# Memory attention of a hybrid streaming layer: scores and prompt values as three float32r passes, the query norm as the exponential's scale

## The chip, the cores and the metric

The kernel runs on one core of a Trainium2 chip. The metric is the device time of one execution in microseconds (us). Shares, windows and chains come from one execution taken by the hardware profiler, whose own time stands beside its span below. Five engines work side by side, each through an instruction stream of its own: PE (TensorE: matrix products and transposes; its weight loads, PEld, are recorded apart), DVE (VectorE), ACT (ScalarE), POOL (GpSimd) and SP (SyncE, which issues the loads and stores). Products are written to banks in PSUM, eight in all; the other engines copy them out to SBUF.

## The reference

One layer serves a prompt of 512 tokens and a sample of 64 tokens with the same weights: a mixer (a gated delta recurrence beside differential attention), then attention over a memory, then a feed-forward part. The change lies in the memory attention:

```python
def _rmsnorm(x, g):
    xf = x.astype(jnp.float32)
    y = xf * lax.rsqrt(jnp.mean(xf * xf, axis=-1, keepdims=True) + EPS)
    return (y * g.astype(jnp.float32)).astype(x.dtype)
...
def _mem_kv(mem, g, wk, wv):
    B, M, _ = mem.shape
    m = _rmsnorm(mem, g)
    return (m @ wk).reshape(B, M, H_MEM, D_MEM), (m @ wv).reshape(B, M, H_MEM, D_MEM)

def _mem_attn(x, mk, mv, wq, wo):
    B, L, _ = x.shape
    q = (x @ wq).reshape(B, L, H_MEM, D_MEM)
    s = jnp.einsum('blhd,bmhd->bhlm', q.astype(jnp.float32), mk.astype(jnp.float32)) * (D_MEM ** -0.5)
    p = jax.nn.softmax(s, axis=-1)
    o = jnp.einsum('bhlm,bmhd->blhd', p, mv.astype(jnp.float32)).astype(x.dtype)
    return o.reshape(B, L, D_MODEL) @ wo
...
    h = x + jnp.concatenate([oa, ob], axis=-1) @ p['w_out']
    h = h + _mem_attn(_rmsnorm(h, p['ln_mem_q']), mem_k, mem_v, p['w_mem_q'], p['w_mem_o'])
    hn = _rmsnorm(h, p['ln_ffn'])
    h = h + jnp.square(jax.nn.relu(hn @ p['w_ff1'])) @ p['w_ff2']
```

The model width is 1024, the memory has 256 tokens, and four heads are 256 wide, so the scores are divided by 16. The prompt attends to memory keys and values that are projected here from `mem_prompt` (they are outputs too). The sample attends to cached ones, `cache_mem_k` and `cache_mem_v`.

## The kernel before

Activations are kept transposed, features on the 128 partitions and the 576 tokens (512 of the prompt, then 64 of the sample) along the free axis. A large tile is a "pair", `u` in the profile: 128 x 2 x 4 x 576 elements. It either holds the high and the low half of one split operand for 512 features, or two unrelated things, which `view` cuts out. `pair(slot)` hands out one of six slots (0 to 5); a slot's next tile waits until the last reader of the one before it is done.

**Split operands.** A large projection is not done in float32 but as three float32r products: the operand is rounded to float32r (the high half), the rest is a float32r number again (the low half), and high x high, high x low and low x high are summed in one bank. For weights `split_weights` (L154) loads a raw block, ACT casts the high half `wh` (L160), DVE subtracts for the low half `wl` (L161). There are three raw buffers and two each of `wh` and `wl`, so weights are split one block ahead of their use. For activations `split_to` (L196) does the same, with a gain per feature as ACT's scale where there is one (L203).

**Projections.** `project` (L168) makes 128 output columns for all tokens in two halves, tokens 0 to 255 and 256 to 575. Per 128 input features the first half takes one 512-wide product of the high weights with the high and low halves of the activations side by side, and one 256-wide product of the low weights; the second half takes three products of 320. Over 1024 features that is 8 x (512 + 256) and 24 x 320 columns. Since the first half leaves its two parts in two halves of a bank, its readout adds them: `add_to` (L192) copies one on ACT (L193) and adds the other on DVE (L194).

**Banks** (L74): three for projections (`pr`), two for transposes and short work (`ba`), one each for `g0`, `g1` and `gs`. Scores use `gs` alone, so the scores of the next tile wait until the exponential of the tile before has read them.

**Around the memory attention,** in program order:
- L1028 to L1058: memory keys and values are projected for 256 memory tokens, in two blocks of 512 columns each. `mkv` holds transposed keys `mkT` and values `mv`, in float32. Keys go to a token-major buffer `mkt` first (L1045), are transposed on PE and copied to `mkT` by ACT (L1054); values go to `mv` directly. Both are stored by DMA from where they stand (L1055).
- L1064 to L1110: the mixer's output projection adds to the residual (`add_residual`, L1071); squares are summed, and at the end `norm_columns` (L1098) makes five columns of inverse roots of the mean squares, one for each tile of 128 queries, by a power on POOL (L207). The gain of the norm is already in the split activations `hx` (L1108), the root is not.
- L1111 and L1112: the root must multiply every query. `row_broadcast` (L209) turns the five columns into a row of 576 on all partitions, `rB`, by five float32 products with the identity (ten records) and two copies. It is handed to the first query projection and put between its two halves (`between`).
- L1115 to L1126: cached keys (`cm`, 1 MB, L1116) and cached values (`cmv`, 1 MB, L1119) are loaded, values first in the built order; the keys are transposed in four groups of four through `ba` and copied to `cmT`, which shares a pair with `cmv`.
- L1128 to L1175: four heads. For each, two query projections with readout `scaled` (query times `rB`, L1137) into `qh`. Then five query tiles: four of the prompt and one that ends on the 64 sample tokens. A tile takes two float32 score products (L1149), maximum along the row on DVE (L1151), times -1/16 (L1152), exponential on ACT with the maximum as bias, 1/16 as scale and the row sum as second output (L1154), reciprocal and scaling on DVE (L1155, L1156), two transposes on PE (L1159), and a copy of each block into `pT`, one by ACT (L1160), one by DVE (L1161). After the five tiles come the values: two float32 products of 512 columns and two of 64 for each of two output blocks, and the split of the results into `mo` (L1174, L1175).
- L1177 on: the output projection of the memory attention, the second norm (with a row of roots of its own before the feed-forward part), and the feed-forward part.

**What sets the order.** The program order above is not the order on the engines. A scheduler places each engine's instructions when the kernel is built, by priority and by when their operands are ready in its own estimate; each engine then runs its list in order and waits at each instruction for what it needs. So the query projections of head h+1 are interleaved with the score tiles and the values of head h, and the output projection with those of head 3. Weight splits have high priority. The entries of the broadcast are pinned. Loads and stores are issued by SP in one queue, in its built order.

In the profile every product stands at L106 (`mm`), every transpose at L112 (`tr`), so tiles tell them apart: `pr` is a projection, `gs` scores, `g` values, `ba` transposes and the broadcast. A float32 product or transpose leaves two records.

## Time and profile before

| what | before |
|---|---|
| median of 3 runs | 1047.21 us (1047.1 to 1047.5) |
| the profiled execution's own time | 1047.51 us |
| its span in the trace | 1045.8 us |
| granted TensorE clock, mean | 0.997 |
| DMA, whole span | 89.96 MB at a mean of 86 GB/s |
| projections' products on high weights | 2680 records, 692.6 us busy |
| projections' products on low weights | 1776 records, 484.5 us busy |
| casts of weights (ACT) and subtractions (DVE) | 153 each, 136.5 and 157.3 us busy |

The profile's page gives busy time by engine, then groups by line, then the chain of work that ended last, followed back from the last instruction. Busy times of neighbouring PE instructions overlap: a record's duration holds its filling and draining, so the distance from one start to the next, the pitch, says what an instruction costs, not its mean duration. The span is 1.7 us shorter than the execution's own time. Views of the trace are given as rows that begin with a time in us from the span's start and a duration; what stands in brackets at the end is the idle time just before and what ended it.

### The profile page before, as it was taken

What the parts mean: (1) busy time and instruction counts of PE and PEld (TensorE: products, weight loads), DVE (VectorE), ACT (ScalarE), POOL (GpSimd) and SP (SyncE); (2) the same over time, 40 slices, a digit from 0 to 9 for tenths busy, and PEclk for the clock granted to TensorE, in tenths of its full rate; (3) what the DMA queues carried; (4) which work ended last, traced back from release to release, by engine and by line L of the source; (5) the groups of instructions that cost most, each with busy time, mean ns of one, the idle gap of its engine ahead of it and who ended that gap; (6) DMA issues with size and microseconds to landing.
All of it is one profiled execution on the core that took longest, in us unless ns stands there. A gap on an engine that the chain in (4) does not pass through costs nothing.

```text
span 1045.8 us, 16809 instructions
## 1 busy us (share of the span) xinstructions
PE 1027.9 (98%) x6520; PEld 928.9 (89%) x6520; DVE 669.1 (64%) x1473; ACT 434.7 (42%) x905; POOL 58.0 (6%) x124
## 2 busy tenths in 40 slices
PE   9999999999999999999999999999999999999996
PEld 7989899998888878998877899999999999999996
DVE  6676784766667675664554666666666666666773
ACT  6644664433465674343333443323232222222344
POOL 3431110100000000000000000000000000000000
PEclk9999999999999999999999999999999999999998
DMA  7432411100321446434111232141413131323312
GB/s 210 129 104 81 122 43 26 37 21 21 92 64 56 157 136 207 135 86 137 41 41 41 67 92 65 48 120 45 121 48 114 51 112 57 108 58 112 92 51 91
DMA packets 139442, 89.96 MB, mean 86 GB/s; under 512 B 5522, under 2 KB 130576, under 8 KB 138852
## 3 DMA queue, kind: packets, MB, share of 16 engines
q1 hardware_dynamic: 138996, 88.24, 28.8%
q8 instruction: 52, 0.85, 0.4%
q10 hardware_dynamic: 368, 0.66, 0.2%
q14 instruction: 26, 0.21, 0.1%
HBM read 79.14 MB, written 9.74 MB: 85 GB/s over the span
## 4 chain that ended last, share of the span: by engine, by line
PE 67%; issue 2%; DVE 0%; ACT 0%; POOL 0%; POOLq 0%; ACTq 0%
PE pr L106 58%; PE g L106 3%; PE gs L106 3%; PE ba L112 2%; PE ba L106 0%; ACT u L1240 0%; POOL tiny L207 0%; DVE u L1076 0%; POOL ta L207 0%; POOLq L1320 0%; DVE an L1008 0%; DVE u L1175 0%; DVE on L779 0%; ACT u L1174 0%; ACT p L1154 0%
## 5 line engine op out<-in xcount | busy, mean ns | idle before, releaser
L106 PE MATMUL pr<-u,wh 128*128 128x320 f32 (+2 forms) x2680 | 692.6, 341 | 1.3 <-DVE p L322 1.0
L106 PEld LDWEIGHTS pr<-u,wh 128*128 128x128 f32 x2680 | 456.8, 188 | 36.2 <-DVE p L322 1.3
L106 PE MATMUL pr<-u,wl 128*128 128x256 f32 (+1 forms) x1776 | 484.5, 300 | 0.0
L106 PEld LDWEIGHTS pr<-u,wl 128*128 128x128 f32 x1776 | 327.1, 189 | 8.1 <-issue 1.4
L160 ACT CAST wh<-raw 128x1024 fp32r<-128x1024 f32 (+1 forms) x153 | 136.5, 892 | 234.9 <-PE pr L106 222.7
L161 DVE TENSOR_TENSOR wl<-raw,wh 128x1024 fp32r<-128x1024 f32 (+1 forms) x153 | 157.3, 1028 | 59.9 <-ACT wh L160 56.8
L1076 DVE TENSOR_TENSOR u<-u,pr 128x256 f32<-128x256 f32 (+1 forms) x160 | 72.4, 453 | 62.5 <-PE pr L106 59.7
L200 ACT CAST u<-p 128x256 fp32r<-128x256 f32 x64 | 27.8, 434 | 51.8 <-DVE p L1194 51.8
L207 POOL TENSOR_TENSOR tiny<-tiny,nhalf 128x1 f32<-128x1 f32 (+4 forms) x11 | 9.4, 852 | 651.4 <-DVE tiny L1256 409.0
L106 PE MATMUL pr<-wh,u 128*128 128x512 f32 x128 | 41.1, 399 | 0.0
L201 DVE TENSOR_TENSOR u<-p,u 128x256 fp32r<-128x256 f32 x64 | 29.2, 457 | 15.1 <-ACT u L200 15.1
L193 ACT COPY p<-pr 128x256 f32<-128x256 f32 (+1 forms) x42 | 15.6, 372 | 49.1 <-PE pr L106 49.1
L1078 DVE TENSOR_TENSOR u<-u,pr 128x256 f32<-128x256 f32 x80 | 33.6, 420 | 2.4
L194 DVE TENSOR_TENSOR p<-pr,p 128x256 f32<-128x256 f32 (+1 forms) x42 | 17.8, 423 | 25.5 <-ACT p L193 25.4
L456 DVE SCALAR_TENSOR_TENSOR p<-p,gcol,p 128x579 f32<-128x579 f32 x33 | 27.1, 821 | 9.0 <-ACT p L454 8.5
L1193 DVE TENSOR_TENSOR p<-pr,rB 128x320 f32<-128x320 f32 x32 | 15.7, 492 | 25.9 <-PE pr L106 25.9
L1194 DVE SCALAR_TENSOR_TENSOR p<-p 128x256 f32<-128x256 f32 x64 | 29.3, 458 | 2.2
L203 ACT ACTIVATE u<-u,gcol 128x256 fp32r<-128x256 f32 (+1 forms) x32 | 17.0, 533 | 31.1 <-DVE u L1078 31.1
L106 PE MATMUL g<-u,qz 128*128 128x256 f32 (+4 forms) x96 | 29.3, 409 | 0.0
L741 ACT COPY X<-g 128x512 f32<-128x512 f32 (+1 forms) x24 | 13.2, 551 | 34.3 <-PE g L112 34.3
L106 PEld LDWEIGHTS pr<-wh,u 128*128 128x128 f32 x128 | 23.4, 188 | 4.4
L106 PE MATMUL gs<-u,aT 128*128 128x128 f32 (+1 forms) x136 | 26.6, 320 | 0.0
(336 smaller groups left out, 1194.1 us busy)
## 6 DMA issues: line engine op xcount, KB each, us to landing
raw<-in_w_ff_dram SPq DMA_DIRECT2D x32, 512.0 KB
raw<-in_w_ff_dram SPq DMA_DIRECT2D x64, 256.0 KB
raw<-in_w_in_dram SPq DMA_DIRECT2D x28, 512.0 KB
raw<-in_w_mem_k_dram SPq DMA_DIRECT2D x8, 512.0 KB
raw<-in_w_mem_v_dram SPq DMA_DIRECT2D x8, 512.0 KB
raw<-in_w_out_dram SPq DMA_DIRECT2D x8, 512.0 KB
raw<-in_w_mem_q_dram SPq DMA_DIRECT2D x8, 512.0 KB
raw<-in_w_mem_o_dram SPq DMA_DIRECT2D x8, 512.0 KB
```

What stands on the lines that cost most here:

```text
L106: i = nc.tensor.matmul(out, lhsT, rhs, start=start, stop=stop)
L112: i = nc.tensor.transpose(out, in_, ident[:n, :n])
L160: A.copy(wh, raw)
L161: V.tensor_tensor(wl, raw, wh.bitcast(F32), ALU.subtract)
L194: V.tensor_tensor(dst, b, dst, ALU.add)
L200: A.copy(h, src)
L201: V.tensor_tensor(lo, src, h.bitcast(F32), ALU.subtract)
L203: A.activation(h, src, AF.Identity, scale=g)
L456: V.scalar_tensor_tensor(yv[:, :n], cb[:, i : i + n], cwt[:, m, i : i + 1], yv[:, :n], ALU.mult, ALU.add)
L1076: V.tensor_tensor(hm, hm, b, ALU.add)
L1078: V.tensor_tensor(hm, hm, more, ALU.add)
L1194: V.scalar_tensor_tensor(f, f, 0.0, f, ALU.max, ALU.mult)
```

## The change

- **Keys and prompt values are split.** The pairs of `mkv` and `cmu` become float32r. Transposed keys of the prompt and of the cache are rounded by ACT and their rest subtracted by DVE (`split_turned`). The low halves of the prompt's keys lie in small tiles that the recurrent stage used (`At0`, `At1`, `Dt0`, `Dt1`), those of the cached keys in the second half of `cmu`. The prompt's values are copied from the token buffer to `mv` (high) and subtracted into four tiles (`Y0`, `Y1` and two of `B1`). Keys and values now both pass through one token buffer, `tokens`.
- **Queries are split and not scaled.** `split_query` adds the two parts of the first half into a short-lived tile `zr`, copies the high half on ACT to `qh` and subtracts the low half on DVE into `ql`.
- **The root goes into the exponential.** The five columns are multiplied by 1/16 and by -1/16 once (`grow16`, `shrink16`). The maximum of a tile is multiplied by its column of `shrink16`, and the exponential takes its column of `grow16` as scale, by a pointer. `row_broadcast` and `rB` go from this stage; the one before the feed-forward part stays.
- **Scores** are six float32r products a tile in place of two float32 ones, for the sample's tile as well.
- **Probabilities** of the prompt are split from the transposes' bank: high by ACT, low by DVE, four instructions where there were two copies. The sample's go to a tile `pS` by one DVE copy and stay float32.
- **Values:** six float32r products of 512 columns per output block in place of two float32 ones; the sample's two products of 64 columns stay float32, against cached values that are now loaded by four DMAs of 256 KB into tiles `X` and `B0` (two each) in place of one of 1 MB.

```diff
--- before.py
+++ after.py
@@ -88,10 +88,10 @@
 
     SHARED = dict(cb="p0", yv="p1", fs="p0", ko="p0", tm="p1", r="on", acc="p1")
 
-    def small(tag, shape, bufs=None):
+    def small(tag, shape, bufs=None, dt=F32):
         tag = SHARED.get(tag, tag)
         bufs = 1 if tag in ("vn", "on", "S") or tag[:-1] in ("At", "Dt", "Y") else 2
-        return sp.tile(shape, F32, tag=tag, name=nm(tag), bufs=bufs)
+        return sp.tile(shape, dt, tag=tag, name=nm(tag), bufs=bufs)
 
     def tiny(shape, tag="tiny", bufs=16):
         return tp.tile(shape, F32, tag=tag, name=nm(tag), bufs=bufs)
@@ -1025,9 +1025,20 @@
         next(sample, None)
 
 
-    mkv = pair(1)
-    mkT, mv, mkt = view(mkv, 0, KT, NMEM), view(mkv, 1, 2, D), view(e3, 1, 2, D)
-    for w, dst, out in ((w_mem_k, mkt, o_mk), (w_mem_v, mv, o_mv)):
+    def lows(*tags):
+
+        return [small(tag, [P, 512], dt=F32R) for tag in tags]
+
+    def split_turned(hi, low, b):
+
+        A.copy(hi, b.rearrange("p (j n) -> p j n", j=2))
+        V.tensor_tensor(low, b.rearrange("p (j n) -> p j n", j=2), hi.bitcast(F32), ALU.subtract)
+
+    mkv = pair(1, F32R)
+    mkT, mv, tokens = view(mkv, 0, KT, NMEM), view(mkv, 1, 2, D), view(e3, 1, 2, D)
+    mkl, mvl = lows("At0", "At1", "Dt0", "Dt1"), lows("Y0", "Y1", "B1", "B1")
+    for w, out in ((w_mem_k, o_mk), (w_mem_v, o_mv)):
+        dst = tokens
         for f in range(2):
             fs = slice(512 * f, 512 * f + 512)
             bs = [bank("pr") for _ in range(2)]
@@ -1043,6 +1054,9 @@
                             )
             for t in range(2):
                 (A.copy if t else V.tensor_copy)(dst[:, t, fs], bs[t])
+                if out is o_mv:
+                    A.copy(mv[:, t, fs], dst[:, t, fs])
+                    V.tensor_tensor(mvl[2 * t + f], dst[:, t, fs], mv[:, t, fs].bitcast(F32), ALU.subtract)
             if out is o_mk:
                 for i in range(2):
                     b = bank()
@@ -1051,7 +1065,7 @@
                         for t in range(2):
                             tr(b[:, j * 256 + t * P : j * 256 + (t + 1) * P], dst[:, t, m * P : (m + 1) * P])
                     m = 4 * f + 2 * i
-                    A.copy(mkT[:, m : m + 2, :], b.rearrange("p (j n) -> p j n", j=2))
+                    split_turned(mkT[:, m : m + 2, :], mkl[m // 2].rearrange("p (j n) -> p j n", j=2), b)
             nc.sync.dma_start(out[0, 0].rearrange("(b p) h d -> p b (h d)", p=P)[:, :, fs], dst[:, :, fs])
             if out is o_mk and f == 0:
                 finish()
@@ -1108,66 +1122,85 @@
     hx = [pair(i, F32R) for i in (4, 3)]
     for m in range(KT):
         project(weights(w_out[0], m * P), (oa, ob), add_residual(m, True, hx, G_Q))
-    cols, rB = norm_columns(), const([P, T], "rB")
-    broadcast = lambda: row_broadcast(cols, rB, pin=True)
+    cols = norm_columns()
+
+    grow16, shrink16 = tiny([P, 5], "ta"), tiny([P, 5], "ta")
+    V.tensor_scalar(grow16, cols, 1.0 / 16, None, ALU.mult)
+    V.tensor_scalar(shrink16, cols, -1.0 / 16, None, ALU.mult)
 
 
     cm = view(pair(5), 0, 2, D)
     nc.sync.dma_start(cm, cache_mem_k[0, 0].rearrange("(b p) h d -> p b (h d)", p=P))
-    cmu = pair(2)
-    cmv = view(cmu, 0, 2, D)
-    nc.sync.dma_start(cmv, cache_mem_v[0, 0].rearrange("(b p) h d -> p b (h d)", p=P))
-    cmT = view(cmu, 1, KT, NMEM)
+    cmu = pair(2, F32R)
+    cmv = [small(tag, [P, 512]) for tag in ("X", "X", "B0", "B0")]
+    for j, cv_ in enumerate(cmv):
+        src_ = cache_mem_v[0, 0, j // 2 * P : (j // 2 + 1) * P].rearrange("p h d -> p (h d)")
+        nc.sync.dma_start(cv_, src_[:, j % 2 * 512 : (j % 2 + 1) * 512])
+    cmT, cml = (view(cmu, i, KT, NMEM) for i in range(2))
+    mkl, cml = ([x.rearrange("p (j n) -> p j n", j=2) for x in mkl], [cml[:, 2 * i : 2 * i + 2, :] for i in range(4)])
     for k2 in range(KT // 2):
         b = bank()
         for kk in range(2):
             for bi in range(2):
                 tr(b[:, kk * 256 + bi * P : kk * 256 + (bi + 1) * P], cm[:, bi, (2 * k2 + kk) * P : (2 * k2 + kk + 1) * P])
-        A.copy(cmT[:, 2 * k2 : 2 * k2 + 2, :], b.rearrange("p (k n) -> p k n", k=2))
+        split_turned(cmT[:, 2 * k2 : 2 * k2 + 2, :], cml[k2], b)
 
     mo = []
     for h in range(H):
-        qh = [small("kd" if h % 2 else "aT", [P, T]) for i in range(2)]
+        qh = [small("kd" if h % 2 else "aT", [P, T], dt=F32R) for i in range(2)]
+        ql = cp.tile([P, 2, T], F32R, tag=f"qz{h % 2}", name=nm("ql"))
         for i in range(2):
-            def scaled(b, a0, n, more):
-                q = qh[i][:, a0 : a0 + n]
+            def split_query(b, a0, n, more):
                 if more is not None:
+                    q = small("zr", [P, 320])[:, :n]
                     add_to(q, b, more)
                     b = q
-                V.tensor_tensor(q, b, rB[:, a0 : a0 + n], ALU.mult)
-
-            project(
-                weights(w_mem_q[0], (2 * h + i) * P), hx, scaled,
-                between=broadcast if h == i == 0 else None,
-            )
-        pT = [small("p1" if h % 2 else "vb", [P, T]) for _ in range(2)]
+                A.copy(qh[i][:, a0 : a0 + n], b)
+                V.tensor_tensor(ql[:, i, a0 : a0 + n], b, qh[i][:, a0 : a0 + n].bitcast(F32), ALU.subtract)
+
+            project(weights(w_mem_q[0], (2 * h + i) * P), hx, split_query)
+
+        pT = [lows(*tags) for tags in ((("p1", "p1"), ("S", "vn")) if h % 2 else (("vb", "vb"), ("KQ", "KQ")))]
+        pS = small("an", [P, 2, DEC])
         for t, (q0, _) in enumerate(QT):
             t0, n = TT[t]
-            kk = mkT if t < 4 else cmT
+            kk, kl = (mkT, mkl) if t < 4 else (cmT, cml)
             b = bank("gs")
             for i in range(2):
-                mm(b[:, :NMEM], qh[i][:, q0 : q0 + P], kk[:, 2 * h + i, :], start=i == 0, stop=i == 1)
+                m, q = 2 * h + i, slice(q0, q0 + P)
+                low_keys = kl[m // 2][:, m % 2, :]
+                mm(b[:, :NMEM], qh[i][:, q], kk[:, m, :], start=i == 0, stop=False)
+                mm(b[:, :NMEM], qh[i][:, q], low_keys, start=False, stop=False)
+                mm(b[:, :NMEM], ql[:, i, q], kk[:, m, :], start=False, stop=i == 1)
             mx, l = tiny([P, 1]), tiny([P, 1])
             V.tensor_reduce(mx, b[:, :NMEM], AX.X, ALU.max)
-            V.tensor_scalar(mx, mx, -1.0 / 16, None, ALU.mult)
+            V.tensor_scalar(mx, mx, shrink16[:, t : t + 1], None, ALU.mult)
             p = small("p0", [P, 512])
-            A.activation(p[:, :NMEM], b[:, :NMEM], AF.Exp, bias=mx, scale=1.0 / 16, accum_out=l)
+            A.activation(p[:, :NMEM], b[:, :NMEM], AF.Exp, bias=mx, scale=grow16[:, t : t + 1], accum_out=l)
             V.reciprocal(l, l)
             V.tensor_scalar(p[:, :NMEM], p[:, :NMEM], l, None, ALU.mult)
             bt = bank()
             for bi in range(2):
                 tr(bt[:, bi * P : (bi + 1) * P], p[:, bi * P : (bi + 1) * P])
-            A.copy(pT[0][:, t0 : t0 + n], bt[:, P - n : P])
-            V.tensor_copy(pT[1][:, t0 : t0 + n], bt[:, 2 * P - n : 2 * P])
+            if t < 4:
+                for bi in range(2):
+                    src, (dh, dl) = bt[:, bi * P : (bi + 1) * P], (x[bi][:, t0 : t0 + n] for x in pT)
+                    A.copy(dh, src)
+                    V.tensor_tensor(dl, src, dh.bitcast(F32), ALU.subtract)
+            else:
+                V.tensor_copy(pS, bt[:, : 2 * P].rearrange("p (b n) -> p b n", b=2)[:, :, P - n :])
         if h % 2 == 0:
             mo.append(pair(4 if h else 5, F32R))
         for i in range(2):
             b, b2 = bank("g0"), bank("g1")
             fs = slice((2 * h + i) * P, (2 * h + i + 1) * P)
             for bi in range(2):
-                mm(b, mv[:, bi, fs], pT[bi][:, :SEQ], start=bi == 0, stop=bi == 1)
+                m = 2 * h + i
+                mm(b, mv[:, bi, fs], pT[0][bi], start=bi == 0, stop=False)
+                mm(b, mv[:, bi, fs], pT[1][bi], start=False, stop=False)
+                mm(b, mvl[2 * bi + m // 4][:, (m % 4) * P : (m % 4 + 1) * P], pT[0][bi], start=False, stop=bi == 1)
             for bi in range(2):
-                mm(b2[:, :DEC], cmv[:, bi, fs], pT[bi][:, SEQ:], start=bi == 0, stop=bi == 1)
+                mm(b2[:, :DEC], cmv[2 * bi + m // 4][:, (m % 4) * P : (m % 4 + 1) * P], pS[:, bi, :], start=bi == 0, stop=bi == 1)
             j = 2 * (h % 2) + i
             for src, ts_ in ((b, slice(0, SEQ)), (b2[:, :DEC], slice(SEQ, T))):
                 dh, dl = (mo[h // 2][:, p, j, ts_] for p in range(2))
```

## The prediction

> **What bounds the kernel now.** I read the page first: its busy shares, then the chain of waits. Both name TensorE.
>
> ```profile
> PE 1027.9 (98%) x6520; PEld 928.9 (89%) x6520; DVE 669.1 (64%) x1473; ACT 434.7 (42%) x905; POOL 58.0 (6%) x124
> PE 67%; issue 2%; DVE 0%; ACT 0%; POOL 0%; POOLq 0%; ACTq 0%
> ```
>
> PE is busy for 98% of the span and holds two thirds of the chain; no other engine holds a whole per cent. So the order of work on PE sets the time, and an edit counts by the PE time it takes out and by the waits it puts between PE instructions.
>
> Then the view of windows over the stage that the diff touches: part of the key and value projections (399 to 411), the start of the attention stage (470.5 to 487.4), head 0, and head 3 with the drain behind it (558.2 to 580.4); the windows of heads 1 and 2 look like that of head 0.
>
> ```profile
> 399.00:411.00 12.00, 12.00 (x55) 9.93 (x54) 5.55 (x5) 5.63 (x7) 0.00 (x0) 1.00 0.69 220
> 470.50:487.40 16.90, 16.85 (x114) 15.43 (x115) 6.20 (x12) 6.20 (x11) 1.17 (x1) 1.00 0.54 182
> 487.40:511.00 23.60, 23.60 (x129) 18.94 (x128) 12.71 (x37) 8.35 (x23) 0.00 (x0) 1.00 0.15 45
> ...
> 558.20:580.40 22.20, 20.60 (x104) 15.25 (x102) 11.43 (x36) 7.34 (x22) 0.00 (x0) 1.00 0.08 24
> ```
>
> Columns after the length: PE, weight loads, DVE, ACT, POOL, granted clock, DMA. PE is full everywhere but in the last window, where 1.6 us stand idle; DVE is half busy, ACT a third, the clock is 1.00. The chain has the first scores of heads 0, 2 and 3 here, so two heads take 47.0 us, one 23.5:
>
> ```profile
> 487.58 0.86 PE gs L106 x4
> ...
> 534.61 0.86 PE gs L106 x4
> 558.24 0.86 PE gs L106 x4
> ```
>
> A pair of float32 score products (four records, since each is recorded as two) takes 0.86 us (the row starts about 0.2 behind the first record). Heads 0 to 2 hide their softmax under the next head's query projection; head 3 has only part of the output projection to hide under.
>
> **The change part by part.** *Scores and prompt values, PE work.* Each float32 product becomes three float32r products. Pitches come from groups and from runs of equal products in the timeline:
>
> ```profile
> L106 PE MATMUL pr<-u,wl 128*128 128x320 f32 x888 | 253.3, 312 | 0.0
> L106 PE MATMUL pr<-u,wl 128*128 128x256 f32 x888 | 231.2, 287 | 0.0
> ```
>
> ```profile
> 19.05 1.12 PE L106 MATMUL pr<-u,wl 128*128 128x256 f32 x8
> 25.88 1.34 PE L106 MATMUL pr<-u,wl 128*128 128x320 f32 x8
> 404.48 0.61 PE L106 MATMUL pr<-wh,u 128*128 128x512 f32 x2
> 405.16 0.61 PE L106 MATMUL pr<-wh,u 128*128 128x512 f32 x2
> 556.49 0.19 PEld L106 LDWEIGHTS g<-vb,u 128*128 128x128 f32 x1 [0.24 <-issue]
> 556.91 0.19 PEld L106 LDWEIGHTS g<-vb,u 128*128 128x128 f32 x1 [0.24 <-issue]
> ```
>
> Eight float32r products of 256 columns, each with weights of its own, span 1.12 us; less one duration (0.287, the second group's mean) that is 7 pitches of 0.12. Of 320 columns it is (1.34 - 0.31)/7 = 0.147. Three of 512 columns start 0.68 apart (404.48 to 405.16; the third has a row of its own between), so 0.227 each. A float32 product of 512 columns has two records 0.42 apart (556.49 to 556.91), so about 0.85. A tile's scores go from 0.86 to 6 x 0.12 = 0.72: 0.14 less. A value product goes from 0.85 to 0.68: 0.17 less. Per head: 5 x 0.14 + 4 x 0.17 = 1.4 us.
>
> [...]
>
> *Waits between PE instructions.* This is how one tile goes on now (head 0, second to third tile), from the timeline:
>
> ```profile
> 490.75 1.13 PE L106 MATMUL gs<-u,aT 128*128 128x256 f32 x4
> 491.72 0.38 PE L112 MATMUL ba<-ident,p 128*128 128x128 f32 x2
> 491.92 0.42 DVE L1151 TENSOR_REDUCE tiny<-gs 128x1 f32<-128x256 f32 x1 [0.64 <-PE gs L106]
> 492.14 0.27 ACT L1160 COPY vb<-ba 128x128 f32<-128x128 f32 x1 [1.44 <-PE ba L112]
> 492.38 0.15 DVE L1152 TENSOR_SCALAR tiny<-tiny 128x1 f32<-128x1 f32 x1
> 492.45 0.28 DVE L1161 COPY vb<-ba 128x128 f32<-128x128 f32 x1
> 492.76 0.48 ACT L1154 ACTIVATE p<-gs,tiny 128x256 f32<-128x256 f32 x1
> 493.39 1.13 PE L106 MATMUL gs<-u,aT 128*128 128x256 f32 x4
> 496.41 0.20 PEld L112 LDWEIGHTS ba<-ident,p 128*128 128x128 f32 x2 [0.29 <-DVE p L1156]
> ```
>
> There is one score bank, so the next scores start once the exponential has read it: start of the exponential plus 0.63. From the end of the scores (490.75 + 0.86 = 491.6) the chain is 0.3 to the maximum, 0.46 to its scaling, about 0.19 to the exponential where ACT is free, 0.63: 1.6 us. PE fills it with projection work. Two things lengthen it. First, in the built order the low half of the previous tile's probabilities, a subtraction that waits for ACT's copy of the high half, stands on DVE between the maximum and its scaling: +0.26 (a 0.28 us row like L1161, overlapped a little). Second, the exponential now takes scale as well as bias by a pointer:
>
> ```profile
> L1089 ACT ACTIVATE zr<-u 128x256 f32<-128x256 f32 x21 | 8.6, 408 | 3.4 <-DVE u L1078 3.4
> L203 ACT ACTIVATE u<-u,gcol 128x256 fp32r<-128x256 f32 x16 | 8.2, 509 | 31.1 <-DVE u L1078 31.1
> ```
>
> With a scale pointer (L203) an activation of 256 columns takes 0.10 longer than without (L1089). Whether a second pointer adds as much no row shows: 0 to 0.10; I take 0.10. [...]
>
> So the chain is about 1.95 instead of 1.6. The built order puts more projection work into it: for heads 0 to 2 the stretches behind the scores of tiles 0 to 3 hold 8 x 0.35 + 2 x 0.147 = 3.1, 12 x 0.147 = 1.76, 10 x 0.147 + 0.23 = 1.70 and 3.0 us (0.35 is 0.12 + 0.23, a step of the first half of a projection). I laid each against its chain, with the weight split (1.05 on ACT, then 1.23 on DVE, rows below) where it stands inside: the first and last chains end about 0.1 behind the fill, the middle two 0.1 to 0.2 behind.
>
> ```profile
> 487.62 1.05 ACT L160 CAST wh<-raw 128x1024 fp32r<-128x1024 f32 x1 [3.15 <-PE pr L106]
> 488.82 1.22 DVE L161 TENSOR_TENSOR wl<-raw,wh 128x1024 fp32r<-128x1024 f32 x1
> ```
>
> The transposes of a tile come 0.59 us after the scores of the next one may start, because DVE must first invert the sum and scale; 496.41 shows that wait where one float32 product stood ahead of them. Four float32r products cover 0.48 of it, so three tiles of a head wait 0.11 each, against one wait of 0.16 now. Waits of a head: about 0.7 against 0.4. Net per head 1.4 - 0.3 = 1.1, and for three heads **3.3**, between 1.8 (each chain 0.12 later) and 4.7 (no wait added and today's 0.16 gone: 3 x 1.56).
>
> *No row of roots.* The five broadcast products with their entry leave PE:
>
> ```profile
> 478.00 0.86 PEld L112 LDWEIGHTS ba<-ident,u 128*128 128x128 f32 x8 [0.34 <-DMA u<-in_cache_mem_k_dram]
> 480.30 0.48 PE L106 MATMUL pr<-u,wh 128*128 128x512 f32 x1
> 480.82 1.35 PE L106 MATMUL ba<-ident,tiny 128*128 128x128 f32 x10
> 482.13 0.39 PE L106 MATMUL pr<-u,wh 128*128 128x512 f32 x1
> 468.64 0.37 SPq L1119 DMA_DIRECT2D u<-in_cache_mem_v_dram  x1
> 470.40 0.37 SPq L1116 DMA_DIRECT2D u<-in_cache_mem_k_dram  x1
> 470.00:478.00 8.00, 8.00 (x54) 7.31 (x53) 3.17 (x6) 2.44 (x5) 1.17 (x1) 1.00 0.92 316
> ```
>
> From 480.30 to 482.13 two projection products (0.23 + 0.12) should stand; so 1.83 - 0.35 = 1.5 us leave. The transposes of the cached keys move 1.8 us ahead (built order: inside the first query projection's second half, about 476.2 instead of 478.0). Today they wait 0.2 to 0.3 us for their load at 478.0, so they can be late. But that load was queued 1.76 us behind 1 MB of cached values; these are now four loads of 256 KB, queued on SP among the input and key weight loads, where their tiles come free from the recurrent stage (behind them stand weights that are held three deep). At 316 GB/s (the last row) a megabyte less is 3.3 us less, so keys land near 474.6 and the wait goes (0.2 gained). The third transpose group now waits for copy and subtraction of the first (0.59 + 0.69 on two engines, one bank of two): 0.2 lost. Sum **+1.45**; bounds 0.5 (keys 1 us late) and 1.7.
>
> *Head 3.* Its fill is the same 6.9 us of output projection, but the built order puts none of it between the fourth and fifth tile. There PE waits the whole chain, 1.95 less 0.1, where today 4 x 0.12 + 3 x 0.23 = 1.2 us of work stands in it and 0.2 us is idle (570.02 below). Behind the fifth tile the first low half is 0.45 late, the high half 0.35. Laid out tile by tile from the head's first scores (about 558.0), the projection resumes after 19.7 us; today:
>
> ```profile
> 570.02 1.13 PE L106 MATMUL gs<-u,kd 128*128 128x256 f32 x4 [0.20 <-ACT p L1154]
> 577.52 0.48 PE L106 MATMUL pr<-u,wh 128*128 128x512 f32 x1
> ```
>
> at 577.52, that is after 19.5. So the 1.4 us of saved work all go into waits: **-0.2**, between -1.0 and +0.6.
>
> *At nothing:* splitting keys and values where they are made (8 subtractions and 4 casts more, each 0.6 to 0.7 us): PE is full in the window of that stage, with DVE at 5.55 and ACT at 5.63 of 12 us, and weights are split one block ahead. Without that cover it would be 4 x 1.3 us. Values now pass through the keys' token buffer, so the second half of the normed activations must wait for the store of the last values; in the built order that store stands behind the first four output weight loads, as today, and the write comes four projections of 8 x 0.35 + 24 x 0.147 = 6.3 us later.
>
> **Sum.** 3.3 + 1.45 - 0.2 = 4.55 us off the profiled execution's 1047.51 (span 1045.8), so 1042.95; the median of the runs is 0.3 lower, so **1042.7 us**. The bounds add to 1.3 and 7.0; as they need not fall together, the forecast's own range is 1040.8 to 1045.
>
> **Rivals.** (a) *Larger gain:* the chains hide wholly, in head 3 too, since ACT and DVE are half idle: 4.7 + 1.45 + 0.6 = 6.75: 1040.5. For it: heads 0 to 2 wait little today. Against it: the chain grows by 0.35 with the low half and the second pointer, and no fill grows with it in head 3.
> (b) *The softmax chain sets the pace of every head*, and saved PE work turns into waits, as I expect for head 3. For it: the chain grows by 0.35 while the scores shrink. Against it: the fills of 1.7 to 3.1 us. Only the broadcast's 1.45 stays: 1045.8, which is within 0.2%.
> (c) *Slower:* ACT now makes two probability copies and the query's high half (L193's copy, then a cast of 0.4) ahead of the exponential in one queue. If on each of 15 tiles one such 0.4 us stands in front of the exponential beyond what I lined up, 6.0 us are lost: 1042.7 + 6.0 = 1048.7. It decides from 4.55/15 = 0.3 us per tile. Against it: ACT is busy 8.35 of 23.6 us.
> (d) *The passes don't run at their pitch*, bound by weight loads of 0.19 us (row 556.49): 120 x 0.07 = 8.4 slower on scores, 1051. The run of eight at 0.12 speaks against it.
>
> **How the numbers follow.** Forecast 0.70, (a) 0.13, (b) 0.11, (c) 0.04, (d) 0.02. The range 1040.2 to 1045.9 holds nearly all of the forecast, half of (a) and what of (b) lies at its 1045.8, and leaves out (c) and (d). A measurement of this kernel tells about 0.2%, 2.1 us, from no change. Faster: forecast and (a), 0.83, and a little of (b): 0.84. Same: 0.10. Slower: (c) and (d), 0.06.
>
> **What would show it.** In the profile after: first scores of successive heads 22.4 us apart; six score records in 0.72; no products with the roots as operand behind the query projection; an exponential of 0.57; key transposes with no wait for their load; in head 3 a PE gap of 1.8 us before the fifth tile. Wrong would be heads still 23.5 apart (b), score products 0.19 apart (d), or PE waiting over 0.5 us for the exponential in most tiles (c).

## The result and the profile after

The changed kernel takes 1042.27 us (median of 4 runs, 1041.22 to 1042.61), the kernel before 1047.24 us beside it: a ratio of 0.9951, with a 95% interval of 0.9939 to 0.9962. In a second set of runs it was 1042.12 against 1047.43 us, 0.9945 (0.9932 to 0.9957). The prediction of 1042.7 lies 0.4 above the first median. The profiled execution took 1041.22 us, which only one other of the nine reached; a second one (label "again") took 1042.38, near the median. Both are read below, because they differ in one place. Their spans in the trace, 1039.2 and 1040.3 us, are 6.6 and 5.5 below that of the kernel before; some 0.3 of that does not reach the executions' own times, which lie 2.0 to 2.1 us above their spans where it was 1.7. No run shows why.

The first profile's page, engines and chain of waits:

```profile
PE 1019.3 (98%) x6566; PEld 931.0 (90%) x6566; DVE 680.0 (65%) x1502; ACT 445.6 (43%) x936; POOL 58.3 (6%) x124
PE 87%; DVE 3%; issue 2%; POOL 2%; ACT 2%; DMA 1%; POOLq 0%; ACTq 0%; DVEq 0%; SPq 0%
```

PE lost 8.6 us of busy time and DVE and ACT each gained 11, which is the trade that was made: products for copies and subtractions. PE still holds most of the chain. The windows (PE, weight loads, DVE, ACT, POOL, clock, DMA) over the keys' and values' projections, a stretch of heads 0 and 1, and head 3:

```profile
399.00:411.00 12.00, 12.00 (x55) 9.92 (x55) 7.08 (x8) 6.57 (x9) 0.00 (x0) 1.00 0.65 221
487.40:511.00 23.60, 23.60 (x152) 21.41 (x151) 14.96 (x44) 10.94 (x31) 0.00 (x0) 1.00 0.16 45
551.30:573.80 22.50, 19.68 (x118) 16.27 (x116) 12.48 (x40) 8.70 (x26) 0.00 (x0) 1.00 0.08 24
```

The keys' and values' splits cost PE nothing (12.00 of 12.00). Heads 0 to 2 stay full; head 3 now stands idle for 2.8 us where it was 1.6. The timeline's rows that mark the stage are the end of the norm's sums, the key transposes and the first scores of heads 0 to 3, then the small stall behind head 3:

```profile
473.92 0.72 PE L106 MATMUL ba<-ones,p 128*128 128x1 f32 x6
476.20 1.03 PE L112 MATMUL ba<-ident,u 128*128 128x128 f32 x8
485.78 0.28 PE L106 MATMUL gs<-u,aT 128*128 128x256 f32 x1
...
507.55 0.28 PE L106 MATMUL gs<-u,kd 128*128 128x256 f32 x1
...
529.46 0.28 PE L106 MATMUL gs<-u,aT 128*128 128x256 f32 x1
...
551.35 0.28 PE L106 MATMUL gs<-u,kd 128*128 128x256 f32 x1
...
573.84 0.56 PE L106 MATMUL pr<-u,wh 128*128 128x320 f32 x2 [0.30 <-DVE u L1090]
```

The same marks in three traces, as differences in us:

| stretch | before | after | again |
|---|---|---|---|
| last sum of the norm to first scores of head 0 | 13.41 | 11.86 | 11.86 |
| heads 0, 1, 2 (first scores to next first scores) | 23.45, 23.57, 23.64 | 21.77, 21.91, 21.89 | 21.78, 21.89, 21.87 |
| head 3, from its first scores to the stall of 0.30 | 22.26 | 22.49 | 23.44 |
| from there to the end | 465.46 | 465.36 | 465.40 |

So 1.55 us left the stretch before head 0, 5.1 us left heads 0 to 2, and head 3 gave back 0.2 us in one execution and 1.2 in the other. The rest of the kernel is the same to 0.1 us. Head 3 is where the two executions part. In the first:

```profile
562.20 0.28 PE L106 MATMUL gs<-u,ql 128*128 128x256 f32 x1
564.05 0.51 PE L106 MATMUL gs<-u,kd 128*128 128x256 f32 x2 [1.57 <-ACT p L1179]
...
565.95 0.50 PE L106 MATMUL g<-S,u 128*128 128x512 f32 x1
566.29 0.39 PE L106 MATMUL g<-p,Y 128*128 128x512 f32 x1
566.52 0.40 PE L106 MATMUL g<-p,u 128*128 128x512 f32 x1
564.40:568.30 3.90, 3.26 (x17) 1.96 (x15) 2.16 (x9) 1.68 (x5) 0.00 (x0) 1.00 0.00 0
```

In the second, the same instructions (timeline, then the same window):

```profile
564.14 0.51 PE L106 MATMUL gs<-u,kd 128*128 128x256 f32 x2 [1.57 <-ACT p L1179]
...
566.65 0.78 PE L106 MATMUL g<-S,u 128*128 128x512 f32 x1
567.22 0.63 PE L106 MATMUL g<-p,Y 128*128 128x512 f32 x1
567.65 0.54 PE L106 MATMUL g<-p,u 128*128 128x512 f32 x1
564.40:568.30 3.90, 3.76 (x14) 2.91 (x14) 1.83 (x7) 1.09 (x4) 0.00 (x0) 0.56 0.00 0
```

Both wait 1.57 us for the exponential of the fourth tile. Behind that wait the value products start 0.34 and 0.23 apart in the first trace and 0.57 and 0.43 in the second, and the granted clock of the window is 1.00 against 0.56. Head 3 is 0.95 us longer for it, out of 1.1 us between the two spans; the other 0.14 us stand already ahead of the norm's last sum (474.06 against 473.92).

### The profile page after: what moved, and what is told of

Same layout as the page of the kernel before. It is cut to its first block, busy times and chain, and to the rows that moved or that the text cites. A ratio compares the mean times of both kernels' runs of the same rounds, so it can differ in the third digit from the quotient of the medians.

```text
span 1039.2 us, 16983 instructions
## 1 busy us (share of the span) xinstructions
PE 1019.3 (98%) x6566; PEld 931.0 (90%) x6566; DVE 680.0 (65%) x1502; ACT 445.6 (43%) x936; POOL 58.3 (6%) x124
## 4 chain that ended last, share of the span: by engine, by line
PE 87%; DVE 3%; issue 2%; POOL 2%; ACT 2%; DMA 1%; POOLq 0%; ACTq 0%; DVEq 0%; SPq 0%
PE pr L106 68%; PE g L106 9%; PE gs L106 5%; PE ba L112 2%; PE g L112 2%; DVE wl L161 0%; PE ba L106 0%; POOL tg L207 0%; DVE p L456 0%; DMA out_dram<-S 0%; DMA S<-in_state_gdn_dram 0%; POOL tiny L207 0%; POOL X L603 0%; DVE on L779 0%; ACT L644 0%
## 5 line engine op out<-in xcount | busy, mean ns | idle before, releaser
L203 ACT ACTIVATE u<-u,gcol 128x256 fp32r<-128x256 f32 (+1 forms) x32 | 17.0, 533 | 30.4 <-DVE u L1092 30.4
L106 PE MATMUL pr<-u,u 128*128 128x320 f32 (+2 forms) x160 | 26.5, 323 | 0.0
```

What stands on the lines that cost most here:

```text
L106: i = nc.tensor.matmul(out, lhsT, rhs, start=start, stop=stop)
L203: A.activation(h, src, AF.Identity, scale=g)
```

## The experiments

Each kernel ran four times or more, beside the kernel before on the same chip. Times are medians. The builder's scheduler orders PE's instructions anew for every kernel: through the four heads only again and long_gap have the order of the change, so in all others a difference holds the edit and a new order together.

**The change again.** No edit.

> The changed kernel as it is, once more, for a second trace and a narrower interval. Its runs so far lie between 1041.22 and 1042.61 us, 1.4 apart, where those of the kernel before lie within 0.4. First theory (the heads are bound by PE's work): the first scores of successive heads again 21.8 to 21.9 us apart, whatever the total, so that what separates the runs lies outside the heads. Second theory (the softmax chains sit just at the limit of PE's fill): a slower run shows heads 22.1 or more apart, with PE waiting for the exponential. Median 1042.3 by both.

1042.12 us. Heads 21.78, 21.89 and 21.87: the first theory. What separates the two executions lies in head 3, as the rows above show.

**The row of roots put back** ("row_kept").

```diff
-    cols = norm_columns()
-    grow16, shrink16 = tiny([P, 5], "ta"), tiny([P, 5], "ta")
...
+    cols, rB = norm_columns(), const([P, T], "rB")
+    broadcast = lambda: row_broadcast(cols, rB, pin=True)
...
+                V.tensor_tensor(q, b, rB[:, a0 : a0 + n], ALU.mult)
...
+            A.activation(p[:, :NMEM], b[:, :NMEM], AF.Exp, bias=mx, scale=1.0 / 16, accum_out=l)
```

> The row of roots is put back: five broadcast products between the halves of the first query projection, the query multiplied by it before it is split, the exponential with 1/16 as a plain scale. All else as changed. First theory: only the broadcast's PE time comes back, 1.55 us by the two traces (487.42 against 485.78, less 0.09 that was there before), heads stay at 21.8, since the exponential's 0.57 us and its 0.48 us without the pointer are both hidden: 1043.8 us. Second theory (chains at the limit): the exponential is shorter by 0.09 in 20 tiles but each query readout has one DVE multiplication more (0.4 to 0.5 us) ahead of the split; if that sets the pace, heads grow by 0.2 or more and the time is 1044.5 or above; if the shorter exponential does, heads shrink and the time is 1042.8 or below.

1042.95 us, 0.8 above the change and 0.9 below what the first theory gave. The trace has the broadcast back (13.26 us before head 0, 1.4 more), but its heads are 21.73, 21.81 and 21.61, 0.4 less in sum, and its head 3 takes 22.12 against 22.49 and 23.44. Shorter heads are the last branch of the second theory. So the root as a scale earns 1.4 us at the broadcast and gives back 0.6, in heads 0 to 2 and in head 3, by the longer exponential or by the other order; the extra DVE multiplication costs nothing that the heads show.

**The norm alone, on the kernel before** ("norm_only"): the counterpart.

```diff
-                V.tensor_tensor(q, b, rB[:, a0 : a0 + n], ALU.mult)
+                else:
+                    V.tensor_copy(q, b)
...
-            V.tensor_scalar(mx, mx, -1.0 / 16, None, ALU.mult)
+            V.tensor_scalar(mx, mx, shrink16[:, t : t + 1], None, ALU.mult)
...
-            A.activation(p[:, :NMEM], b[:, :NMEM], AF.Exp, bias=mx, scale=1.0 / 16, accum_out=l)
+            A.activation(p[:, :NMEM], b[:, :NMEM], AF.Exp, bias=mx, scale=grow16[:, t : t + 1], accum_out=l)
```

> The kernel before with one part of the change alone: the root as the exponential's scale, no row of roots; scores and values stay float32, probabilities are copied and not split. First theory: the broadcast's 1.46 us leave PE (row_kept against the second trace of the changed kernel: 487.38 against 485.92), heads stay at 23.45 to 23.64: 1047.4 - 1.5 = 1045.9 us. If the parts add, heads must already be shorter here: scores_only has 22.2 and values_only 22.7, which with 21.85 for both would make 22.2 + 22.7 - 21.85 = 23.05 for neither; then 1044.4 us. Heads at 23.5 would say that the values' split is worth 0.85 next to float32 scores and 0.35 next to split ones, that is, that a wait takes half of it there.

1046.53 us against 1047.29, a ratio of 0.9992 (0.9983 to 1.0001): 0.8 us, half of the expected 1.5, and not clear of nothing by itself. The trace has 12.01 us before head 0 (1.4 less), heads of 23.49, 23.55 and 23.70 as before, and 0.2 us more in head 3. So the part is worth about 0.8 us on either kernel. In this trace 0.2 of the missing 0.6 us is found in head 3, and about 0.1 lies outside the span (own time less span: 1.86 us in the median of its runs, 1.78 in those of the kernel before); the rest isn't accounted for.

**One part left float32.** With float32 values ("scores_only") the score tiles stay split, with float32 scores ("values_only") the values do.

```diff
-                mm(b, mv[:, bi, fs], pT[0][bi], start=bi == 0, stop=False)
-                mm(b, mv[:, bi, fs], pT[1][bi], start=False, stop=False)
-                mm(b, mvl[2 * bi + m // 4][:, (m % 4) * P : (m % 4 + 1) * P], pT[0][bi], start=False, stop=bi == 1)
+                mm(b, mv[2 * bi + m // 4][:, (m % 4) * P : (m % 4 + 1) * P], pT[bi], start=bi == 0, stop=bi == 1)
```

> Values go back to float32: two products of 512 columns an output block, probabilities copied and not split. Scores stay split, the root stays the exponential's scale. First theory: each head gets back its value products' time, 0.76 us by the traces (4.71 against 3.95 us of PE time at the value products of head 0), so heads 22.5 to 22.6 apart, and head 3 gets 0.4 to 0.7 of it: 1042.3 + 2.3 + 0.5 = 1045.1 us. Second theory (softmax chains pace the heads): the four probability splits a tile go too, so the chains are shorter and most of the products' time is given back: heads at most 22.2, 1043.5 us or less.

```diff
-                mm(b[:, :NMEM], qh[i][:, q], kk[:, m, :], start=i == 0, stop=False)
-                mm(b[:, :NMEM], qh[i][:, q], low_keys, start=False, stop=False)
-                mm(b[:, :NMEM], ql[:, i, q], kk[:, m, :], start=False, stop=i == 1)
+                mm(b[:, :NMEM], qh[i][:, q], kk[m // 2][:, m % 2, :], start=i == 0, stop=i == 1)
```

> Scores go back to float32: two products a tile, queries and keys not split. Prompt values stay split, the root stays the exponential's scale. First theory: each head gets back 0.79 us (6.15 against 5.36 us of PE time at scores and transposes of head 0), heads 22.5 to 22.6 apart; in head 3, where PE stands idle for 1.57 us ahead of the fifth tile, at most half comes back: 1042.3 + 2.4 + 0.3 = 1045.0 us. Second theory (chains pace the heads): the query's split, 0.4 us on ACT and 0.4 to 0.5 on DVE for each half, is off the engines and the scores' 0.14 us a tile lie in waits: heads at most 22.2, 1043.5 us or less.

1043.96 and 1043.62 us. Float32 values lengthen the heads to 22.13, 22.25 and 22.19, 0.33 on average, about half of the products' own time: the second theory's side for the heads, though the total lies between the two theories (in this trace head 3 takes 23.92 us, part of it at a granted clock of 0.50 behind a wait of 1.41 us). Float32 scores lengthen them to 22.59, 22.63 and 22.92, 0.85 each: the first theory. Yet values_only comes out below the 1045.0 expected, because its head 3 takes 21.81 us in place of 22.49 or 23.44; the builder's order put projection work ahead of the fifth tile there, and PE waits 0.19 instead of 1.57 (timeline of values_only):

```profile
565.75 1.13 PE L106 MATMUL gs<-u,kd 128*128 128x256 f32 x4 [0.19 <-ACT p L1175]
```

**The pointers taken away** ("plain_scale").

```diff
-            V.tensor_scalar(mx, mx, shrink16[:, t : t + 1], None, ALU.mult)
+            V.tensor_scalar(mx, mx, -1.0 / 16, None, ALU.mult)
...
-            A.activation(p[:, :NMEM], b[:, :NMEM], AF.Exp, bias=mx, scale=grow16[:, t : t + 1], accum_out=l)
+            A.activation(p[:, :NMEM], b[:, :NMEM], AF.Exp, bias=mx, scale=1.0 / 16, accum_out=l)
```

> The changed kernel with 1/16 as a plain scale of the exponential and -1/16 as plain factor on the maximum: the norm's root is left out of the scores, everything else stays. First theory (chains have cover in heads 0 to 2): heads stay within 0.15 of 21.85, the exponential takes 0.48 in place of 0.57, and head 3's tail gets 0.1 to 0.15 shorter for each of its three waits for a chain, 0.3 to 0.4 in all: about 1041.8 us. Second theory (the pointer sets the pace): 15 times 0.09 to 0.15 more, 1040.3 us or less.

1039.94 us, 2.2 below the change; the time is that of the second theory. The kernel leaves the norm's root out and serves only to price the pointers. The second theory's mechanism is not there: heads are 21.77, 21.82 and 22.00, no shorter without the pointers. Nearly all the gain is in head 3 (21.49 us to the stall). There the builder's order has changed too, with the wait before the fifth tile at 1.01 us, so the total does not price the pointers by themselves; it shows again that head 3 decides. One chain can be priced: from the start of head 3's fourth maximum to the fifth tile's scores it is 1.53 us with the pointers (562.52 to 564.05 in the first trace of the change) and 1.44 without, here (561.47 to 562.91) and in row_kept (563.47 to 564.91). The runs agree within 0.55 us.

**Banks for the scores.** "last_bank" puts the fifth tile's scores in g1, "two_banks" the second and fourth tile's.

```diff
-            b = bank("gs")
+            b = bank("g1" if t == 4 else "gs")
```

> The changed kernel with the fifth tile's scores in bank g1 in place of gs, so that they need not wait for the fourth tile's exponential. In both traces PE stood idle for 1.57 us there, in head 3; in the second trace the granted clock was 0.56 in the 3.9 us behind it, in the first 1.00, and these two differ by 0.94 us in head 3's tail and by nothing else. First theory (the idle stretch costs its length, and at times a slow clock behind it that makes the spread of the runs): PE idles under 0.8 us at once in the tail, the clock stays at 1.00, the tail is 18.5 to 19.2 us in place of 19.83 and 20.77, runs agree within 0.5 us, and the time is 1042.1 - 1.4 = 1040.7 us. Second theory (the softmax chain of tiles 4 and 5 sets head 3's end whatever the bank): the wait moves to the transposes, the tail stays at 19.5 or above, 1041.7 us or more.

```diff
-            b = bank("gs")
+            b = bank("g1" if t % 2 else "gs")
```

> As last_bank, but tiles 2 and 4 of every head have their scores in g1 and tiles 1, 3 and 5 in gs, so no scores wait for the exponential right before them. First theory: heads 0 to 2 gain only what they still wait, under 0.2 each (21.65 to 21.85), since PE is full there; the tail of head 3 is 18.5 to 19.2; 1040.5 us, runs within 0.5. Second theory (chains pace the heads): heads shrink to 21.3 or less and the time is 1039.3 or less. Third: g1 also holds the sample's products, and their late readout holds back the next head's second scores: heads 22 or more.

last_bank takes 1041.33 us (1040.50 to 1042.71), between the theories, and its runs are as far apart as before. The wait went elsewhere: the fifth tile's scores run early, and PE now waits for the fourth tile's probabilities (timeline of last_bank).

```profile
564.77 0.44 PE L112 MATMUL ba<-ident,p 128*128 128x128 f32 x2 [1.34 <-DVE p L1181]
```

two_banks takes 1036.70 us (1036.54 to 1037.15): 0.9900 of the kernel before (0.9887 to 0.9914) and 5.4 us below the change, far more than expected. Heads 0 to 2 are hardly shorter (21.74, 21.71, 21.93). It is head 3 again, here from its first scores until the output projection runs alone, in a window of two_banks:

```profile
551.32 0.28 PE L106 MATMUL gs<-u,kd 128*128 128x256 f32 x1
551.30:569.20 17.90, 17.90 (x119) 16.36 (x117) 12.19 (x40) 8.58 (x27) 0.00 (x0) 1.00 0.11 31
```

No idle time is left and the clock stays at 1.00. The expectation had counted the waits that stand in brackets (some 2.8 us); the trace adds that starts were also late by 0.1 to 0.3 us at many products without such a mark (565.95 to 566.29 above is 0.34 where 0.23 would do), and head 3 of again paid 0.95 us at a clock of 0.56. From head 3's first scores to the end two_banks needs 1034.5 - 551.32 = 483.2 us, the first trace of the change 487.9, the second 488.8. The builder also put head 3's projection products in other places, so what the bank is worth without the new order was not tried.

**What the banks do without the change, and what the change is worth with them.** "before_two_banks" is the bank edit on the kernel before; the other two put float32 values or float32 scores into two_banks.

> The kernel before with nothing of the change, but with the scores of tiles 2 and 4 of each head in bank g1. First theory (head 3's waits are there in the kernel before as well and cost about what they cost in the changed one): heads stay at 23.3 to 23.6, head 3's tail loses its waits, 1047.3 - 4.5 = 1042.8 us, and with it the change would be worth 1042.8 - 1036.7 = 6.1 us between kernels with two score banks, more than the 5.2 between kernels with one. Second theory (the waits in head 3 come from the longer chain of the change): at most 1.5 us off, 1045.8 or more.

> Two score banks, split scores, float32 values (probabilities copied). Where PE never waits, the products' own time must show in full. First theory: 8 value blocks with two float32 products of 0.85 against six of 0.232, 0.32 us each: 1036.7 + 2.6 = 1039.3 us; the 0.35 us a head that the values' split was worth next to one score bank was the rest after a wait. Second theory (the split's own cost on ACT, DVE and in PE's order eats half of it wherever it stands): 4 x 0.35, 1038.1 us or less.

> Two score banks, float32 scores, split values. First theory: 20 tiles at 0.14 to 0.16 us of PE time: 1036.7 + 3.0 = 1039.7 us. Second theory (float32 scores need no query split and shorten what DVE and ACT do, which paced head 3): 1038.5 us or less.

1044.15, 1039.22 and 1040.54 us. The banks alone give the kernel before 3.2 us, between the two theories (4.5 and at most 1.5), so its head 3 had waits of its own, though fewer. Between kernels with two banks the change is worth 1044.15 - 1036.70 = 7.5 us, where it was 5.0 and 5.3 between kernels with one. Float32 values cost 2.5 us there, as the first theory has it to 0.1; float32 scores cost 3.8, more than the 3.0 expected. By heads (means of three): 23.44 before, 22.56 with split values, 22.45 with split scores, 21.79 with both. Split values are worth 0.65 next to split scores and 0.88 next to float32 ones, split scores 0.77 and 0.99.

**A longer wait** ("long_gap"). PE's order is the changed kernel's.

```diff
             p = small("p0", [P, 512])
+            if h == 3 and t == 3:
+                for _ in range(5):
+                    A.copy(p[:, :NMEM], b[:, :NMEM])
```

> The changed kernel with five more copies on ACT (256 columns, about 0.4 us each, written where the exponential writes over them) ahead of the exponential of head 3's fourth tile, PE's order unchanged. The stretch in which PE waits ahead of the fifth tile grows from 1.57 to about 3 us. First theory (a wait of this length is what lowers the granted clock behind it, by chance at 1.57 us, surely at 3): the window behind the wait has a granted clock near 0.56 for some 4 us, the products in it start 0.4 us or more apart in place of 0.23, and the time is 1041.3 + 1.5 + 1.0 to 1.8 = 1043.8 to 1044.6 us, runs close together. Second theory (the 0.56 of the second trace has nothing to do with the wait): clock 1.00 behind the wait, and 1042.1 + 1.5 = 1043.6 us or less, with runs 1.4 apart as before.

1043.88 us (1043.22 to 1045.03). The wait grew to 3.26 us, and the clock behind it fell, as the timeline and the windows of long_gap show:

```profile
565.89 0.51 PE L106 MATMUL gs<-u,kd 128*128 128x256 f32 x2 [3.26 <-ACT p L1182]
...
568.24 0.78 PE L106 MATMUL g<-S,u 128*128 128x512 f32 x1
568.82 0.63 PE L106 MATMUL g<-p,Y 128*128 128x512 f32 x1
...
565.60:566.60 1.00, 0.71 (x5) 0.71 (x6) 0.52 (x2) 0.23 (x2) 0.00 (x0) 0.93 0.00 0
566.60:567.60 1.00, 0.91 (x5) 0.61 (x3) 0.05 (x1) 0.27 (x1) 0.00 (x0) 0.50 0.00 0
567.60:568.60 1.00, 0.95 (x2) 0.66 (x3) 0.79 (x4) 0.40 (x2) 0.00 (x0) 0.50 0.00 0
568.60:569.60 1.00, 1.00 (x3) 0.79 (x3) 0.70 (x3) 0.43 (x2) 0.00 (x0) 0.50 0.00 0
569.60:570.60 1.00, 1.00 (x5) 0.57 (x3) 0.01 (x1) 0.17 (x1) 0.00 (x0) 0.87 0.00 0
```

The clock is 0.50 in three whole windows, 0.93 and 0.87 in those at their sides. Counted as parts at 0.50 and at 1.00, that is 0.50 for about 3.4 us (0.14 us of the first window, three whole ones, 0.26 of the last), from some 0.6 us after PE has work again: an estimate from these windows. Its five runs have mean clocks of 0.993 to 0.996, those of two_banks 0.997 throughout. That the runs would lie close together, as the first theory had it, is a miss: they are 1.8 us apart.

## Why the prediction was right, and where it was not

The total came out within 0.5 us, partly by luck: heads 0 to 2 gained 1.8 us more than forecast, head 3 lost up to 1.0 us more, and 0.3 us of the shorter span did not reach the time.

- **No row of roots: 1.45 forecast, 1.55 measured** at its place (13.41 to 11.86). The transposes start at 476.20, as laid out, with no wait for their load. But the part as a whole is worth only 0.8 us (norm_only, row_kept): 0.2 to 0.4 us comes back in head 3 in both traces. The pointers make one chain 0.09 us longer (1.53 against 1.44, above), which head 3 pays where PE stands idle behind it; how much of the rest is the builder's new order was not settled.
- **Heads 0 to 2: 3.3 forecast, 5.1 measured**, above the bound of 4.7. The PE work of 1.4 us a head was right. A score pair costs 0.86 and six products at 0.118 cost 0.71; a value product costs 0.86 (two records 0.429 apart) and three at 0.233 cost 0.70; the rest of PE's list in a head is the same in both kernels. So 5 x 0.15 + 4 x 0.16 = 1.4. A change from float32 to float32r costs nothing beside that, though one row looks like it (values_only, end of the first scores of head 0):

```profile
485.85 1.02 PE L106 MATMUL gs<-At,aT 128*128 128x256 f32 x4
486.52 0.58 PE L106 MATMUL pr<-u,wh 128*128 128x512 f32 x1
486.94 0.28 PE L106 MATMUL pr<-u,wl 128*128 128x256 f32 x1
```

  The product at 486.52 lasts 0.42 to the next start instead of 0.235. But from 485.85 to 486.94 it is 1.09 us, and four float32 records at 0.214 with one product at 0.235 are 1.09: the rest of the last float32 record stands under the product behind it.
- **The step that failed is the waits, forecast to grow from 0.4 to 0.7 us a head; they shrank.** A head is 1.7 us shorter, 0.3 more than its work. Take from each head its products at their usual pitch (0.118, 0.147 and 0.233 us for float32r products of 256, 320 and 512 columns, 0.216 and 0.429 for a float32 record of 256 and 512, 0.109 for a transpose's, 0.112 for a 64-column product's; a record of these float32r products lasts 0.287, 0.312 and 0.402 in the groups of the kernel before, each 0.17 longer than its pitch). What is left, summed over all of a head's starts, are late starts: 1.14 us a head before, 0.87 after, 0.27 less where 0.3 more was forecast (the forecast's 0.4 had counted only part of them). By place, late starts of the transposes grew from 0.11 to 0.24, about as forecast (0.16 to 0.33), and those of the projections from 0.05 to 0.18; but those of the scores fell from 0.56 to 0.33 and those of the values from 0.43 to 0.13.

  Why they fell is open. Between two-bank kernels each split is worth its work when the other group is split already (values 0.65 of 0.64, scores 0.77 of 0.75) and 0.23 more when the other is still float32, so whichever split comes first takes late starts with it. With one bank float32 values lengthen a head by only 0.33, because the late starts of scores_only come to 0.56. The builder's order of PE differs in all of these, and no run keeps it fixed.

  For the scores two things can be read. All waits for the single bank come to under 0.1 us a head: with one bank the heads take 21.85, with two 21.79. And the chain is shorter than the 1.95 laid out. This is the second tile's in the first trace of the change:

```profile
490.53 0.28 PE L106 MATMUL gs<-u,ql 128*128 128x256 f32 x1
...
490.85 0.42 DVE L1176 TENSOR_REDUCE tiny<-gs 128x1 f32<-128x256 f32 x1 [0.43 <-PE gs L106]
491.19 0.28 DVE L1189 TENSOR_TENSOR KQ<-ba,vb 128x128 fp32r<-128x128 f32 x1
491.38 0.20 DVE L1177 TENSOR_SCALAR tiny<-tiny,ta 128x1 f32<-128x1 f32 x1
491.67 0.57 ACT L1179 ACTIVATE p<-gs,tiny,ta 128x256 f32<-128x256 f32 x1
492.40 0.36 PE L106 MATMUL gs<-u,aT 128*128 128x256 f32 x1
```

  The low half does stand between the maximum and its scaling, but the scaling starts 0.53 after the maximum where it was 0.46: 0.07 more, not 0.26. The low half starts 0.08 before the maximum's row ends, and the scaling 0.09 before the low half's ends. The exponential takes 0.57, 0.09 more than 0.48, where 0.10 was taken from the rows of L203 and L1089. From the end of the scores (490.53 + 0.12) to the next ones it is 1.75 us, and the twelve projection products in it last 1.76: the chain lies hidden to the last tenth.
- **Head 3: +0.2 forecast, +0.2 in one execution and +1.2 in the other.** The wait before the fifth tile was forecast at 1.8 and is 1.57. That the clock would be 0.56 over the 3.9 us behind such a wait, as in the second execution, was not in the sum. How often it is stays open: the median of the nine runs lies 0.9 us above the fastest, but only two were traced, and the run of 1042.14 us has the mean clock of the first trace, 0.998, where again has 0.996, so a slow clock is not all that separates the runs.
- **At nothing:** right; the window of the keys and values is full and the time up to the norm's sums is the same to 0.1 us.

Of the rivals, (a) came nearest for the heads, 4.7 us against 5.1: their score chains hide. Its other half, no wait in head 3, is what two_banks then reached. (b) is true of head 3 alone. (c) and (d) are out: no wait above 0.5 us stands before the scores of heads 0 to 2, and six score products take 0.71 (485.78 to 486.49).

The values' split saved 0.65 us a head between two-bank kernels, a fifth of the 3.4 that four float32 products take at 0.86; the forecast had 4 x 0.17 = 0.68 from the rows.

## What to carry to other kernels

Cutting PE work paid in full where PE was full (heads 0 to 2: 1.7 us a head for 1.4 of work); the same cut in a stretch where a chain through one bank sets the pace went into waits (head 3: 0.2 us longer or more), so lay out the last block, which has no successor to hide under, apart from the others. A second bank for alternate tiles, borrowed from a tag that holds only the sample's products, was worth more here (5.4 us, with the order that the builder made for it) than the whole change (5.0), and it made the change itself worth 7.5. To price a split, separate the work from the late starts first: the work came out to 0.1 us a head, the late starts moved the other way. And look at a second execution before reading a difference of a tenth of a per cent from one trace: here the first trace was one of the two fastest of nine.

## What the runs showed of the hardware

Behind a wait of 1.57 us in head 3 the granted clock was 1.00 in one execution of the change and 0.56 over 3.9 us in another ("again"), with the same instructions. Narrower windows, of again and then of scores_only, where PE waited 1.41 us until 565.17 and 0.24 us until 566.60:

```profile
564.10:564.60 0.50, 0.46 (x3) 0.46 (x4) 0.45 (x2) 0.00 (x0) 0.00 (x0) 0.94 0.00 0
564.60:565.60 1.00, 1.00 (x7) 1.00 (x5) 0.07 (x1) 0.00 (x0) 0.00 (x0) 0.50 0.00 0
565.60:566.60 1.00, 0.86 (x3) 0.31 (x2) 0.65 (x3) 0.27 (x1) 0.00 (x0) 0.50 0.00 0
566.60:567.60 1.00, 1.00 (x3) 0.84 (x3) 0.52 (x3) 0.82 (x3) 0.00 (x0) 0.50 0.00 0
567.60:568.60 1.00, 1.00 (x6) 0.78 (x4) 0.39 (x2) 0.00 (x0) 0.00 (x0) 0.82 0.00 0
...
565.20:566.20 1.00, 1.00 (x8) 0.96 (x8) 0.47 (x2) 0.00 (x0) 0.00 (x0) 1.00 0.00 0
566.20:567.20 1.00, 0.76 (x4) 0.37 (x3) 0.74 (x3) 0.29 (x2) 0.00 (x0) 0.97 0.00 0
567.20:568.20 1.00, 1.00 (x3) 0.48 (x2) 0.30 (x2) 0.63 (x2) 0.00 (x0) 0.50 0.00 0
568.20:569.20 1.00, 1.00 (x2) 0.32 (x2) 0.21 (x1) 0.00 (x0) 0.00 (x0) 0.50 0.00 0
569.20:570.20 1.00, 1.00 (x3) 0.23 (x1) 0.00 (x0) 0.29 (x1) 0.00 (x0) 0.50 0.00 0
570.20:571.20 1.00, 0.62 (x5) 0.52 (x4) 0.87 (x2) 0.29 (x1) 0.00 (x0) 0.82 0.00 0
```

By the estimate made for long_gap, the clock was 0.50 for about 3.4 us in again, scores_only and long_gap (behind a wait of 3.26 us). That began 0.4 us after PE had work again behind the long wait in again, 0.6 in long_gap and 2.0 in scores_only. In again and long_gap the products of 512 columns in that stretch started 0.42 to 0.59 apart, against 0.23 at a clock of 1.00. Behind the waits of row_kept (1.36 us), last_bank (1.34) and plain_scale (1.01) the windows up to 576 hold a clock of 1.00. What parts the first trace of the change from again was not shown.
